# Strassen products for a pair of tiles in the last FFN chunks of a two-layer encoder

## Chip, cores and metric

One core of one Trainium2 chip. The metric is the device time of one launch in microseconds. Its engines are named as in the profile: PE (TensorE) multiplies, PEld is its weight load, DVE (VectorE) and ACT (ScalarE) work on elements, POOL (GpSimd) and SP (SyncE) issue DMA transfers among other things.

## What is computed

An inference step of an encoder with two layers. Each layer has a mixer and then a channel MLP with squared ReLU, which is the part that matters here:

```python
for i in range(DEPTH):                     # 2 layers
    ...
    h = rmsnorm(x, g_norm[i, 2]) * (1 + sc2) + sh2
    f = jnp.square(jax.nn.relu(h @ ffn_w_up[i])) @ ffn_w_down[i]
    x = x + gt2 * rmsnorm(f, g_norm[i, 3])
```

`x` has 1024 prompt rows and 32 sample rows of 1024 channels; `ffn_w_up` is 1024 x 4096 and `ffn_w_down` 4096 x 1024, in float32. The outputs are the new rows and the states of the mixers.

## The kernel before

**Tiles.** The rows lie along the free dimension in three tiles (`TILES`, L27): tiles 0 and 1 with 384 columns each, tile 2 with 256 prompt and 32 sample columns, 288 together. Channels lie on partitions, in 8 blocks of 128.

**Three products.** Each float32 operand is split into a rounded part and its remainder (`wh`, `wl` for weights, `hh`, `hl` for the input, `fh`, `fl` for the hidden part). A product of 128 x 128 weights is three matmuls: wh by the rounded input, wh by the remainder, wl by the rounded input (`products`, L929).

**Chunks and passes.** The MLP's 4096 hidden channels are cut into eight chunks of 512. `passes` (L338 to L345) lists which chunk is worked on for which tiles. In a pass, a tile has four up products of 8 blocks (96 matmuls, bank `pf`), relu and square on ACT into `r`, the split into `fh` on ACT and `fl` on DVE, and then eight down products of 4 blocks (96 matmuls, bank `pg`), each added to `acc` on DVE (`ffn_item`, L1358). The downs of one item run after the first up of the next, so PE has work while the hidden part is made. In the second layer, chunks 0 to 3 are done for one tile after the other, 4 and 5 for all three, 6 and 7 for tiles 0 and 1, and 6 and 7 of tile 2 last.

**Weights.** A chunk has eight weight items of 512 KB, four up and four down. SP loads an item into one of three `raw` buffers (`RAW_SLOTS`, L30); `do_w` (L441) copies it on ACT to `wh` and subtracts on DVE into `wl`. Both lie in slots of a ring with the tag W (`W_SLOTS`, 16 slots, so eight items). An item is prepared when the item eight before it is used up (`stream_ready`, L622). Loads of the conditioning weights, "ada", share the stream and the `raw` buffers; DVE multiplies and adds them (`aa`), and `some_ada` (L349) says how many go with which pass.

**Order around it.** The program is written out in Python: `tick` keeps an estimate of PE's time, and `weave`, `pull` and `fillers` interleave the norms, the pool mixer and the output with the passes. A scheduler then orders the instructions of each engine; each engine runs its own list in order, and SP and POOL issue their DMAs in theirs. `mix_to_ffn` (L1455) makes a tile's MLP input. `to_out` (L1659) adds the last residual of tiles 0 and 1, transposes them (`turn_out`) and stores them in 64 pieces of 48 KB (`store_out`, L1649): 40 from SP, 24 from POOL. The last statistics, the transposes and the stores of tile 2 follow its last down products.

## Time and profile before

| | |
|---|---|
| time, median of 3 runs | 2150.81 us (2150.66 to 2152.59) |
| profiled execution, span | 2150.9 us |
| mean granted TensorE clock | 0.998 |
| PE busy | 2133.6 us, 99% |
| DVE busy | 1434.0 us, 67% |
| ACT busy | 976.4 us, 45% |
| DMA | 311.79 MB, mean 145 GB/s |

The span runs from the first to the last instruction of the profiled execution. A row of a group gives source line, engine, operation, output and inputs, shape and count, then the busy time and the mean length of one in ns, then the idle time before them and what ended it. A row of the timeline gives start, length, engine, line and operation. Matmuls overlap in the array, so their lengths add up to more than the time that they take. Lengths on DVE and ACT overlap a little too where neighbours are independent.

### The profile page before, as it was taken

The numbers are of one execution on the slowest core, as the hardware profiler recorded it, in microseconds if no ns is written. First come the engines' busy times: TensorE is split into PE (matmuls) and PEld (weight loads), VectorE is DVE, ScalarE is ACT, GpSimd is POOL, SyncE is SP. The second block draws the span as 40 slices with busy tenths as digits, with TensorE's granted clock in tenths as the row PEclk, the third lists the DMA queues.
The fourth block names the chain that finished last, engine by engine and source line by source line (L and its number), as shares of the span: only waits on it lengthen the run. The fifth ranks groups of instructions, "written<-read, shape, count | busy, mean of one in ns | idle before, by whom it ended". The sixth has DMA issues, their size and how long they took to land.

```text
span 2150.9 us, 33133 instructions
## 1 busy us (share of the span) xinstructions
PE 2133.6 (99%) x13122; PEld 2071.0 (96%) x13122; DVE 1434.0 (67%) x2554; ACT 976.4 (45%) x1655; POOL 22.3 (1%) x44
## 2 busy tenths in 40 slices
PE   8999999999999999999999999999999999999998
PEld 5878999999999999999999999999999999999998
DVE  6778838567778549486757779869675554523377
ACT  5634431233456652323345566666564542313344
POOL 0000000000000000000000000000000000000003
PEclk9999999999999999999999999999999999999999
DMA  8586524353446444244545466565544542302246
GB/s 290 162 262 207 183 82 136 97 157 104 133 126 217 132 148 147 86 131 131 179 125 162 150 184 189 162 197 156 151 145 147 161 153 66 101 20 79 69 127 141
DMA packets 389360, 311.79 MB, mean 145 GB/s; under 512 B 47150, under 2 KB 352598, under 8 KB 389204
## 3 DMA queue, kind: packets, MB, share of 16 engines
q1 hardware_dynamic: 388276, 308.38, 46.9%
q8 instruction: 103, 1.69, 0.3%
q0 software_dynamic: 896, 1.28, 0.3%
q14 instruction: 53, 0.43, 0.1%
q10 hardware_dynamic: 32, 0.01, 0.0%
HBM read 278.95 MB, written 30.66 MB: 144 GB/s over the span
## 4 chain that ended last, share of the span: by engine, by line
PE 97%; DVE 1%; DMA 1%; ACT 0%; issue 0%; DVEq 0%; ACTq 0%
PE pf L934 11%; PE pf L936 11%; PE pg L934 11%; PE pf L935 11%; PE pg L935 11%; PE pg L936 11%; PE pu L934 3%; PE pu L936 3%; PE pu L935 3%; PE po L935 3%; PE po L934 3%; PE po L936 3%; PE pv L960 2%; PE pv L962 2%; PE pv L961 2%; PE psp L1288 1%
## 5 line engine op out<-in xcount | busy, mean ns | idle before, releaser
L934 PE MATMUL pg<-fh,wh_dn 128*128 128x384 f32 (+1 forms) x1536 | 495.6, 323 | 0.1
L934 PE MATMUL pf<-hh,wh_up 128*128 128x384 f32 (+1 forms) x1536 | 494.4, 322 | 0.0
L936 PE MATMUL pf<-hh,wl_up 128*128 128x384 f32 (+1 forms) x1536 | 493.0, 321 | 1.1 <-DVE wl_up L79 1.1
L935 PE MATMUL pf<-hl,wh_up 128*128 128x384 f32 (+1 forms) x1536 | 493.1, 321 | 0.0
L935 PE MATMUL pg<-fl,wh_dn 128*128 128x384 f32 (+1 forms) x1536 | 492.8, 321 | 0.0
L936 PE MATMUL pg<-fh,wl_dn 128*128 128x384 f32 (+1 forms) x1536 | 492.5, 321 | 0.0
L79 DVE TENSOR_TENSOR wl_up<-raw,wh_up 128x1024 fp32r<-128x1024 f32 x152 | 185.5, 1222 | 167.2 <-ACT wh_up L449 167.1
L936 PEld LDWEIGHTS pf<-hh,wl_up 128*128 128x128 f32 x1536 | 288.6, 188 | 1.7 <-DVE wl_up L79 1.7
L934 PEld LDWEIGHTS pg<-fh,wh_dn 128*128 128x128 f32 x1536 | 288.3, 188 | 1.8 <-ACT fh L1194 0.6
L935 PEld LDWEIGHTS pg<-fl,wh_dn 128*128 128x128 f32 x1536 | 288.3, 188 | 1.1 <-DVE fl L79 0.3
L935 PEld LDWEIGHTS pf<-hl,wh_up 128*128 128x128 f32 x1536 | 288.3, 188 | 0.4
L934 PEld LDWEIGHTS pf<-hh,wh_up 128*128 128x128 f32 x1536 | 288.2, 188 | 0.4
L449 ACT ACTIVATE wh_up<-raw 128x1024 fp32r<-128x1024 f32 x152 | 161.1, 1060 | 280.6 <-PE pf L935 214.3
L936 PEld LDWEIGHTS pg<-fh,wl_dn 128*128 128x128 f32 x1536 | 288.3, 188 | 0.0
L79 DVE TENSOR_TENSOR acc<-acc,pg 128x384 f32<-128x384 f32 (+1 forms) x336 | 173.6, 517 | 142.7 <-PE pg L936 142.3
L449 ACT ACTIVATE wh_dn<-raw 128x1024 fp32r<-128x1024 f32 x152 | 160.9, 1060 | 203.5 <-PE pg L935 170.6
L79 DVE TENSOR_TENSOR wl_dn<-raw,wh_dn 128x1024 fp32r<-128x1024 f32 x152 | 185.8, 1223 | 82.8 <-ACT wh_dn L449 82.3
L79 DVE SCALAR_TENSOR_TENSOR aa<-raw,csil,aa 128x512 f32<-128x512 f32 (+1 forms) x364 | 203.7, 618 | 5.4 <-DMA raw<-in_w_ada_dram 5.3
L1370 ACT ACTIVATE r<-pf 128x384 f32<-128x384 f32 (+1 forms) x192 | 86.5, 450 | 201.4 <-PE pf L936 182.2
L79 DVE TENSOR_TENSOR fl<-r,fh 128x384 fp32r<-128x384 f32 (+1 forms) x192 | 99.9, 520 | 82.5 <-ACT fh L1194 81.4
L934 PE MATMUL pu<-hh,wh_u 128*128 128x384 f32 (+1 forms) x384 | 126.0, 328 | 0.0
L934 PE MATMUL po<-ush,wh_o 128*128 128x384 f32 (+1 forms) x384 | 123.5, 322 | 0.0
(273 smaller groups left out, 2923.4 us busy)
## 6 DMA issues: line engine op xcount, KB each, us to landing
raw<-in_ffn_w_up_dram SPq DMA_DIRECT2D x152, 512.0 KB, 3.8
raw<-in_ffn_w_down_dram SPq DMA_DIRECT2D x152, 512.0 KB, 3.4
raw<-in_w_ada_dram SPq DMA_DIRECT2D x96, 512.0 KB, 4.1
raw<-in_sgu_w_in_dram SPq DMA_DIRECT2D x40, 512.0 KB, 3.8
xd<-acc SPq DMA_DIRECT2D x8, 1536.0 KB, 7.4
raw<-in_sgu_w_out_dram SPq DMA_DIRECT2D x24, 512.0 KB, 3.5
xo_r<-xd SPq DMA_DIRECT2D x32, 384.0 KB, 3.4
vd<-vt SPq DMA_DIRECT2D x32, 256.0 KB, 4.4
```

Source lines behind the costliest of these rows:

```text
L79: return op(out, *args, **kw)
L449: act(out=wh, in_=r, func=AF.Copy)
L934: mm(ps[:, :n], wh, rh, start=i == 0, stop=False)
L935: mm(ps[:, :n], wh, rl, start=False, stop=False)
L936: mm(ps[:, :n], wl, rh, start=False, stop=i == last)
L960: mm(ps[:m, :], a_h, wh[:, o : o + 512], start=k == 0, stop=False)
L961: mm(ps[:m, :], a_h, wl[:, o : o + 512], start=False, stop=False)
L962: mm(ps[:m, :], a_l, wh[:, o : o + 512], start=False, stop=k == KB - 1)
L1288: mm(sp[:, c * P : (c + 1) * P], vl[:, c, k * P : (k + 1) * P], wr[:, c * P : (c + 1) * P], start=True, stop=True,)
L1370: act(out=r[:, :n], in_=ps[:, :n], func=AF.Relu)
```

## The change

In the second layer, chunks 4 to 7 of tiles 0 and 1 become four passes of their own (`PAIR`), and tile 2 does all its eight chunks alone, last.

In a paired pass the up products are computed as a product of 2 x 2 blocks. The weights are cut into halves along the 1024 input channels and into two hidden blocks of 128; the two tiles are the two column blocks. Instead of eight block products of 12 matmuls there are seven (Strassen's scheme in Winograd's form), for two hidden block pairs per pass. `quad_product` is one product; four of its right sides are combinations of the tiles' inputs, made once by `combos` and `first_combo` on DVE and ACT; four left sides are combinations of weights, made from two raw items by `quads` (sums on DVE, the split on ACT and DVE; `A22` and the two halves of `S34` in parts of 512). Some products are added up in the same bank, with ACT copying out what stands there in between (`copy`: a1, a2, a3, b1), and DVE adds the parts (`r12`, `r22`, `r11`) before relu and square (`keep`). The down products are as before.

Four of the 16 weight slots are lent (`LENT`) from the last but one single pass of tile 1 on to hold combinations; other combinations take the room of tile 2's input, which is therefore made only during the down products of the last pair pass (`late_norm`). Tile 2's chunks 4 and 5 load their weights again. The ada items that went with the passes of several tiles now go with tile 1's passes 0 to 3, two each. The first layer's order stays.

```diff
@@ -27,6 +27,7 @@
 TILES = [(0, 384, 0), (384, 384, 0), (768, 256, DEC)]
 NT = len(TILES)
 W_SLOTS = 16
+LENT = 4
 RAW_SLOTS = 3
 WINDOWS = (2, 4, 8, 16)
 
...
@@ -258,6 +259,40 @@
 
 
     ada_last = {}
+
+    slots = deque(range(LENT - W_SLOTS, LENT))
+    slots.rotate(LENT)
+    lent = {"left": LENT, "called": False}
+    held = {}
+    ring = []
+
+    def w_tile(name, key=None):
+
+        i = slots.popleft()
+        if key is None:
+            slots.append(i)
+        else:
+            held.setdefault(key, []).append(i)
+        if i < 0:
+            dtype = F32 if key is None else F32R
+            return work.tile([P, 1024], dtype, tag="W", bufs=W_SLOTS - LENT, name=name)
+        dtype = F32 if key is None else F32R
+        if ring[:1] != [dtype]:
+            ring[:] = dtype, work.tile([P, LENT * 1024], dtype, tag="R", bufs=1, name=f"ring{len(ring)}")
+        return ring[1][:, i * 1024 : (i + 1) * 1024]
+
+    def w_free(key):
+        for i in held.pop(key):
+            if i >= 0 and lent["called"]:
+                lent["left"] -= 1
+            else:
+                slots.append(i)
+
+    def w_call():
+        lent["called"] = True
+        for i in [i for i in slots if i >= 0]:
+            slots.remove(i)
+            lent["left"] -= 1
 
     def add_wide(l, j):
 
...
@@ -315,13 +350,14 @@
                 )
 
     def w_chunk(n):
-        l, c, _ = passes[n]
+        l, c, tiles = passes[n]
         for j in range(4):
             f = 4 * c + j
             add_w(
                 ("up", n, j),
                 ffn_w_up[l][:, f * P : (f + 1) * P].rearrange("(k p) f -> p k f", p=P),
                 (8, P),
+                ("one", "two")[j % 2] if tiles == PAIR else "w",
             )
         for q in range(4):
             add_w(
@@ -338,11 +374,11 @@
     passes = [(0, c, [t]) for t in every for c in (0, 1)]
     passes += [(0, c, every) for c in range(2, 4)]
     passes += [(0, c, [t]) for t in every for c in range(4, 8)]
-    passes += [(1, c, [t]) for t in every for c in range(4)]
-    passes += [(1, c, every) for c in range(4, 6)]
-
-    passes += [(1, c, every[:-1]) for c in (6, 7)]
-    passes += [(1, c, [NT - 1]) for c in (6, 7)]
+    PAIR = every[:2]
+    passes += [(1, c, [t]) for t in PAIR for c in range(4)]
+    LEND_AT = ("up", len(passes) - 2, 0)
+    passes += [(1, c, PAIR) for c in range(4, 8)]
+    passes += [(1, c, [NT - 1]) for c in range(8)]
 
     rest = []
 
@@ -383,13 +419,15 @@
         w_chunk(n)
         if l == 0:
             some_ada(12 if len(tiles) > 1 else 4 if c in (4, 5) and tiles == every[:1] else 0)
-        elif len(tiles) > 1:
-            some_ada(4)
+        elif tiles == [1]:
+            some_ada(2)
     some_ada(99)
 
-    worder = [s[1] for s in stream if s[0] == "w"]
+    worder = [s[1] for s in stream if s[0] in ("w", "one", "two")]
     wpos = {k: i for i, k in enumerate(worder)}
-    wdone = set()
+    for _, key, _, _ in [s for s in stream if s[0] == "two"]:
+        for x in ("A1", "A22", "S12", "S34"):
+            wpos[("up", key[1], key[2] // 2, x)] = wpos[key]
     raws = {}
     loads = {}
     state = {"issued": 0, "next": 0, "raw": 0, "used": 0, "folds": 0}
...
@@ -438,10 +476,57 @@
             loads[key] = i.ins
             state["issued"] += 1
 
+    def w_pair(key, w=1024):
+        names = ["_".join(map(str, (x, *key))) for x in ("wh", "wl")]
+        if w == 512:
+            x = w_tile(names[0], key)
+            witem[key] = x[:, :512], x[:, 512:]
+        else:
+            witem[key] = tuple(w_tile(x, key) for x in names)
+        return witem[key]
+
+    def w_split(key, r, w=1024):
+        wh, wl = w_pair(key, w)
+        act(out=wh, in_=r, func=AF.Copy)
+        tt(out=wl, in0=r, in1=wh.bitcast(F32), op=ALU.subtract)
+
+    def quads(n, j, r1, r2):
+
+        a11, a12, a21, a22 = r1[:, :512], r1[:, 512:], r2[:, :512], r2[:, 512:]
+        key = lambda x: ("up", n, j // 2, x)
+        s3 = []
+
+        def first():
+            s3.append(work.tile([P, 512], F32, tag="aa", bufs=2, name=f"s3_{n}_{j}"))
+            tt(out=s3[0], in0=a11, in1=a21, op=ALU.subtract)
+            w_split(key("A1"), r1)
+
+        def second():
+            tt(out=a21, in0=a21, in1=a22, op=ALU.add)
+            w_split(key("A22"), a22, 512)
+
+        def third():
+            tt(out=a22, in0=a21, in1=a11, op=ALU.subtract)
+            w_split(key("S12"), r2)
+
+        def fourth():
+            tt(out=a12, in0=a12, in1=a22, op=ALU.subtract)
+            state["raw"] -= 1
+            wh, wl = w_pair(key("S34"))
+            for at, x in ((0, s3[0]), (512, a12)):
+                w = slice(at, at + 512)
+                act(out=wh[:, w], in_=x, func=AF.Copy)
+                tt(out=wl[:, w], in0=x, in1=wh[:, w].bitcast(F32), op=ALU.subtract)
+            state["raw"] -= 1
+
+        subs.extend([(2, first), (1, second), (2, third), (2, fourth)])
+
+    subs = deque()
+
     def do_w(key, r):
-        wh = work.tile([P, 1024], F32R, tag="W", bufs=W_SLOTS, name="wh_" + "_".join(map(str, key)))
-        wl = work.tile([P, 1024], F32R, tag="W", bufs=W_SLOTS, name="wl_" + "_".join(map(str, key)))
-        witem[key] = (wh, wl)
+        wh, wl = w_pair(key)
+        if key == LEND_AT:
+            w_call()
         if key == ("v", 0, 0):
             act(out=wh[:, :512], in_=r[:, :512], func=AF.Copy)
             late_hi.append(lambda: act(out=wh[:, 512:], in_=r[:, 512:], func=AF.Copy))
...
@@ -1411,6 +1506,122 @@
         pending.append(down)
 
 
+    def pair_item(p, after):
+        l, c, tiles = passes[p]
+        n = ncol[0]
+        hid = {t: [None] * 4 for t in tiles}
+        made = [0]
+
+        def keep(t, j, r, src=None):
+            if src is None:
+                src = r
+            act(out=r, in_=src, func=AF.Relu)
+            act(out=r, in_=r, func=AF.Square)
+            name = f"{l}_{c}_{t}_{j}"
+            if made[0] < 5:
+                a, b = t_hid("h", "fh" + name), t_hid("l", "fl" + name)
+            else:
+                x = work.tile([P, 768], F32R, tag="x3", bufs=3, name="fx" + name)
+                a, b = x[:, :n], x[:, n:]
+            made[0] += 1
+            split(a, b, r, n)
+            hid[t][j] = a, b
+
+        def parts(x):
+            if x > 0:
+                return combo[x]
+            t, k0 = {-11: (0, 0), -21: (0, HK), -22: (1, HK)}[x]
+            return [(hh[t][:, k0 + k, :], hl[t][:, k0 + k, :]) for k in range(HK)]
+
+        def quad_product(ps, jp, w, x, first):
+            key, at = w
+            wh, wl = need_w(("up", p, jp, key))
+            tick(12 * (0.004 + n / 2265.0))
+            for k, (rh, rl) in enumerate(parts(x)):
+                o = slice(at + k * P, at + (k + 1) * P)
+                mm(ps[:, :n], wh[:, o], rh, start=first and k == 0, stop=False, skip_group_check=True)
+                mm(ps[:, :n], wh[:, o], rl, start=False, stop=False, skip_group_check=True)
+                mm(ps[:, :n], wl[:, o], rh, start=False, stop=k == HK - 1, skip_group_check=True)
+
+        def copy(ps, name):
+            x = t_c(name)
+            act(out=x, in_=ps[:, :n], func=AF.Copy)
+            return x
+
+        def add(a, b, name):
+            r = t_m(name)
+            tt(out=r, in0=a[:, :n], in1=b[:, :n], op=ALU.add)
+            return r
+
+        def up(jp):
+            name = f"{l}_{c}_{jp}"
+            j = 2 * jp
+
+            def done(key):
+                w_finish(("up", p, jp, key))
+
+            pa, pb = ps_ms(f"pfa{name}"), ps_up(f"pfb{name}")
+            quad_product(pa, jp, ("A1", 0), -11, True)
+            a1 = copy(pa, f"a1{name}")
+            weave()
+            if jp == 0:
+                flush()
+                finish("combos")
+            quad_product(pb, jp, ("S12", 0), 1, True)
+            b1 = copy(pb, f"b1{name}")
+            weave()
+            quad_product(pa, jp, ("S12", 512), 2, False)
+            done("S12")
+            a2 = copy(pa, f"a2{name}")
+            weave()
+            quad_product(pb, jp, ("S34", 512), -22, False)
+            keep(1, j, add(a2, pb, f"r12{name}"))
+            weave()
+            quad_product(pa, jp, ("S34", 0), 3, False)
+            done("S34")
+            a3 = copy(pa, f"a3{name}")
+            keep(1, j + 1, add(a3, b1, f"r22{name}"))
+            weave()
+            pc = ps_up(f"pfc{name}")
+            quad_product(pc, jp, ("A1", 512), -21, True)
+            done("A1")
+            keep(0, j, add(a1, pc, f"r11{name}"))
+            weave()
+            quad_product(pa, jp, ("A22", 0), 4, False)
+            done("A22")
+            keep(0, j + 1, t_m(f"r21{name}"), pa[:, :n])
+            weave()
+
+        def down():
+            sts = {}
+            for q in range(4):
+                wh, wl = need_w(("dn", p, q))
+                for t in reversed(tiles):
+                    for d in (2 * q, 2 * q + 1):
+                        ps = ps_dn(f"pg{l}_{c}_{t}_{d}")
+                        terms = []
+                        for j in (0, 1, 3, 2) if t == 1 else range(4):
+                            o = j * 256 + (d % 2) * P
+                            a, b = hid[t][j]
+                            terms.append((wh[:, o : o + P], wl[:, o : o + P], a[:, :n], b[:, :n]))
+                        products(ps, n, terms)
+                        accumulate(t, d, ps, False)
+                        if after is not None:
+                            if d == 0:
+                                sts[t] = Stat(t, f"rf{l}_{t}")
+                            sts[t].square(d)
+                        if d % 2 == 1 and t == tiles[0]:
+                            w_finish(("dn", p, q))
+                        weave(d % 2)
+            for t in tiles if after is not None else ():
+                after(sts[t])
+
+        up(0)
+        up(1)
+        if after is not None:
+            fillers.append(late_norm.pop())
+        down()
+
     last_ps = {}
 
     def rows_last(part, name):
@@ -1461,7 +1672,76 @@
             for a in range(4):
                 nc.sync.dma_start(xtd[:, a], acc[t][32 * a : 32 * a + 32, :, HALO:])
         need_ada(l, 4)
+        if l == 1 and t == NT - 1:
+            got = []
+            yield from out[0].finish(got)
+            late_norm.append((f"ffn1_{t}", apply(t, 1, 2, 3, got[0])))
+            fillers.append(("combos", combos()))
+            return
         yield from modulate(out[0], l, 2, 3)
+
+    late_norm = []
+    combo = {}
+    HK = KB // 2
+
+    def both(t, k):
+
+        return hh[t][:, k : k + 2, :].bitcast(F32), hl[t][:, k : k + 2, :].bitcast(F32)
+
+    def t_two(name):
+        return t_x(name, [P, 768]).rearrange("p (k n) -> p k n", k=2)
+
+    def keep_parts(x, out):
+        for i, (h, l) in enumerate(out):
+            act(out=h, in_=x[:, i, :], func=AF.Copy)
+            tt(out=l, in0=x[:, i, :], in1=h.bitcast(F32), op=ALU.subtract)
+
+    def combos():
+
+        while lent["left"]:
+            yield 1.0
+        units = []
+        for tag, n in (("R", 5), ("hh2", 3), ("hl2", 3)):
+            x = work.tile([P, n, 2, 384], F32R, tag=tag, bufs=1, name=f"combo_{tag}")
+            units += [(x[:, i, 0], x[:, i, 1]) for i in range(n)]
+        units.append(
+            (
+                work.tile([P, 384], F32R, tag="rr", bufs=2, name="combo_rr"),
+                late.tile([P, 384], F32R, tag="wg", bufs=1, name="combo_wg"),
+            )
+        )
+        for i in (2, 3, 4):
+            combo[i] = units[4 * i - 8 : 4 * i - 4]
+        combo[1] = [(hh[1][:, k], hl[1][:, k]) for k in range(HK)]
+        for k in (0, 2):
+            x, y, z = (t_two(f"combo_{v}{k}") for v in "xyz")
+            tt(out=x, in0=both(1, k)[0], in1=both(1, k)[1], op=ALU.add)
+            tt(out=y, in0=both(1, HK + k)[0], in1=both(1, HK + k)[1], op=ALU.add)
+            yield True
+            tt(out=z, in0=y, in1=x, op=ALU.subtract)
+            keep_parts(z, combo[3][k : k + 2])
+            yield True
+            tt(out=z, in0=both(0, k)[0], in1=both(0, k)[1], op=ALU.add)
+            tt(out=x, in0=x, in1=z, op=ALU.subtract)
+            yield True
+            tt(out=y, in0=y, in1=x, op=ALU.subtract)
+            keep_parts(y, combo[2][k : k + 2])
+            yield True
+            tt(out=z, in0=both(0, HK + k)[0], in1=both(0, HK + k)[1], op=ALU.add)
+            tt(out=z, in0=z, in1=y, op=ALU.subtract)
+            keep_parts(z, combo[4][k : k + 2])
+            yield False
+
+    def first_combo():
+
+        for k in (0, 2):
+            x, z = (t_two(f"combo1_{v}{k}") for v in "xz")
+            tt(out=x, in0=both(1, k)[0], in1=both(1, k)[1], op=ALU.add)
+            tt(out=z, in0=both(0, k)[0], in1=both(0, k)[1], op=ALU.add)
+            yield True
+            tt(out=x, in0=x, in1=z, op=ALU.subtract)
+            keep_parts(x, combo[1][k : k + 2])
+            yield False
 
     def to_ffn0(st):
         fillers.append((f"ffn0_{st.t}", mix_to_ffn(st, 0)))
...
@@ -1624,12 +1904,24 @@
         for p, (pl, c, tiles) in enumerate(passes):
             if pl != l:
                 continue
+            if tiles == PAIR:
+                if p > 0 and passes[p - 1][2] != PAIR:
+                    paired()
+                pair_item(p, after if c == 7 else None)
+                continue
             for t in tiles:
                 if c == 0:
                     if any(f[0] == f"ffn{l}_{t}" for f in fillers):
                         flush()
                     finish(f"ffn{l}_{t}")
                 ffn_item(p, t, after if c == 7 else None)
+
+    def paired():
+
+        def stages():
+            yield from first_combo()
+
+        fillers.append(("combos", stages()))
 
     run_ffn(0, to_pool)
 
```

More of the change, by code (lines that the diff above doesn't have):

```diff
@@ L239, in tile_stream_encoder_step, with add_w @@
     witem = {}
-    def add_w(key, ap, shape):
-        stream.append(("w", key, ap, shape))
+    def add_w(key, ap, shape, kind="w"):
+        stream.append((kind, key, ap, shape))
     def add_ada(l, j):
@@ L424, in issue @@
             else:
-                r = work.tile([P, 1024], F32, tag="W", bufs=W_SLOTS, name=f"raw{k}")
+                r = w_tile(f"raw{k}")
             if kind == "x" and key < 6:
@@ L625, in stream_ready @@
             return False
-        if stream[k][0] == "w":
-            i = wpos[stream[k][1]] - W_SLOTS // 2
-            return i < 0 or worder[i] in wdone
-        return True
+        if subs:
+            return len(slots) >= subs[0][0]
+        return stream[k][0] not in ("w", "one", "two") or len(slots) >= 2
     def stream_step():
+        if not subs and stream[state["next"]][0] == "one":
+            issue()
+            state["next"] += 1
         k = state["next"]
@@ L636, in stream_step @@
         run_deferred()
+        if kind == "two":
+            if not subs:
+                quads(key[1], key[2], raws.pop(k - 1), raws.pop(k))
+            subs.popleft()[1]()
+            if not subs:
+                state["next"] += 1
+            issue()
+            return
         r = raws.pop(k)
@@ L656, in stream_waits @@
         kind, key = stream[state["next"]][:2]
-        if kind == "w":
+        if kind in ("w", "one", "two"):
             return bool(fillers) and wpos[key] > state["used"] + 5 and time["dve"] > time["pe"] + 1.0
@@ L675, in w_finish @@
     def w_finish(key):
-        wdone.add(key)
+        w_free(key)
     fillers = deque()
```

1 line of the change is left out of this document (added).

## The prediction

> **What bounds the kernel now.** I read the page's first two parts, then the windows of the second layer, then the timeline of single matmuls.
>
> ```profile
> span 2150.9 us, 33133 instructions
> PE 2133.6 (99%) x13122; PEld 2071.0 (96%) x13122; DVE 1434.0 (67%) x2554; ACT 976.4 (45%) x1655; POOL 22.3 (1%) x44
> PEclk9999999999999999999999999999999999999999
> PE 97%; DVE 1%; DMA 1%; ACT 0%; issue 0%; DVEq 0%; ACTq 0%
> ```
>
> The chain that ended last is TensorE's at full clock. Each window's columns are its length, the busy times of PE, PEld, DVE, ACT and POOL, then the clock, the DMA share and GB/s:
>
> ```profile
> 1500.00:1600.00 100.00, 99.88 (x563) 97.44 (x562) 69.27 (x126) 56.83 (x100) 0.00 (x0) 1.00 0.53 159
> 1600.00:1700.00 100.00, 100.00 (x635) 100.00 (x634) 58.15 (x90) 51.59 (x86) 0.00 (x0) 1.00 0.47 143
> 1900.00:2000.00 100.00, 100.00 (x624) 100.00 (x623) 31.47 (x48) 29.03 (x49) 0.00 (x0) 1.00 0.16 49
> 2000.00:2100.00 100.00, 100.00 (x600) 100.00 (x599) 58.99 (x93) 46.02 (x76) 0.00 (x0) 1.00 0.39 110
> ```
>
> PE is full, so no wait is left there to gain from, and a new wait adds its whole length. VectorE and ScalarE have a third to two thirds free.
>
> The length of one matmul is no price: matmuls overlap. One 384-column matmul is shown as 335 ns, but the distance between starts is what counts:
>
> ```profile
> L934 PE MATMUL pf<-hh,wh_up 128*128 128x384 f32 x1024 | 343.1, 335 | 0.0
> ...
> 1572.27 0.33 PE L934 MATMUL pf<-hh,wh_up 128*128 128x384 f32 x1
> ...
> 1579.90 0.33 PE L936 MATMUL pf<-hh,wl_up 128*128 128x384 f32 x1
> ...
> 2094.99 0.30 PE L934 MATMUL pf<-hh,wh_up 128*128 128x288 f32 x1
> ...
> 2096.99 0.29 PE L934 MATMUL pf<-hh,wh_up 128*128 128x288 f32 x1
> ```
>
> Start to start it is 44 steps in 7.63 us, 0.1734 us, for 384 columns; for tile 2's 288 columns 15 steps in 2.00 us, 0.1333 us.
>
> **What goes from TensorE.** A plain pass has 96 up matmuls per tile, 192 for two tiles. A paired pass has two halves of seven products of 12 matmuls, 168. Four passes save 4 x 24 = 96 matmuls of 384 columns, 96 x 0.1734 = **16.65 us**. (By the 335 ns it would be 32 us, which counts the overlap twice.) Tile 2's matmuls are moved, not changed: 0. The last norm and its stores still follow tile 2's last product with the same instructions: 0.
>
> The Trainium skill, "TensorE: Matmul & The Clock Gate", part 1, puts the start-to-start time of a warm matmul at N / 2.4 GHz + about 2.5 ns, 162.5 ns for 384 columns. The row's 173.4 ns does not agree, and decides; by the page the saving would be an estimated 15.6 us.
>
> **What is added on the other engines.** Here too the distance between starts is shorter than the shown length, where the next instruction does not need the last one's result:
>
> ```profile
> 1434.66 0.55 DVE L79 TENSOR_TENSOR fl<-r,fh 128x384 fp32r<-128x384 f32 x1
> 1435.13 1.22 DVE L79 TENSOR_TENSOR wl_up<-raw,wh_up 128x1024 fp32r<-128x1024 f32 x1
> 1436.27 0.75 DVE L79 TENSOR_TENSOR sq_r_2x<-sq_r_2x 128x576 f32<-128x576 f32 x1
> 1436.94 1.22 DVE L79 TENSOR_TENSOR wl_up<-raw,wh_up 128x1024 fp32r<-128x1024 f32 x1
> ...
> 1435.68 1.06 ACT L449 ACTIVATE wh_up<-raw 128x1024 fp32r<-128x1024 f32 x1 [0.22 <-PE pf L935]
> 1436.65 0.47 ACT L1370 ACTIVATE r<-pf 128x384 f32<-128x384 f32 x1
> 1437.15 0.52 ACT L1372 ACTIVATE r<-r 128x384 f32<-128x384 f32 x1
> 1437.71 0.52 ACT L1194 ACTIVATE fh<-r 128x384 fp32r<-128x384 f32 x1
> 1438.13 0.56 ACT L1617 ACTIVATE acc<-pp,vec 128x384 f32<-128x384 f32 x1
> ```
>
> DVE: 0.47 us for 384 elements, 1.14 for 1024, 0.67 for 576. ACT: 0.97 for 1024, 0.42 for 384 when independent, 0.5 to 0.56 when it needs the one before. No row shows 512 elements of these kinds: I take 0.60 on DVE and 0.53 on ACT (bounds 0.47 to 0.67 and 0.42 to 0.97). 768 on DVE lies between 0.67 and 1.14; I take 0.87.
>
> DVE gains 16 weight remainders (1.14), 56 half-weight sums and remainders (0.60), 40 additions and remainders of 384 (0.47) and 22 sums of 768 (0.87): 18 + 34 + 19 + 19 = 90 us. ACT gains 16 copies of 1024 (0.97), 24 of 512 (0.53) and 48 of 384 (about 0.45): 16 + 13 + 22 = 51 us. In the four windows above DVE is idle for 182 of 400 us and ACT for 216, so the sums fit; their cost is 0 unless something is late where PE needs it. Sixteen more loads of 512 KB, since tile 2 reads chunks 4 and 5 again, fall into windows with a DMA share of 0.16 to 0.53: 0 as well. Eight ada blocks moved into tile 1's passes 0 to 3 and the 12 instead of 16 weight slots from pass 2 on: the built order puts them just in time there (the latest weight remainder ends within 0.2 us of the matmul that reads it). 0, upper bound 2 us for one load coming late (loads and stores with their time to landing, then SP's timeline with the stores' start and length):
>
> ```profile
> raw<-in_ffn_w_up_dram SPq DMA_DIRECT2D x152, 512.0 KB, 3.8
> raw<-in_ffn_w_down_dram SPq DMA_DIRECT2D x152, 512.0 KB, 3.4
> out_dram<-y_sq SPq DMA_DIRECT2D x33, 48.0 KB, 2.1
> ...
> 2118.13 26.38 SPq L1657 DMA_DIRECT2D out_dram<-y_sq  x40
> ```
>
> **The new waits, place by place.** I listed the instructions of each engine in the built order of the changed kernel, and for each matmul that waits I added what stands ahead on the engine it waits for. A hand-over is read from four rows:
>
> ```profile
> 1800.99 0.33 PE L936 MATMUL pg<-fh,wl_dn 128*128 128x384 f32 x1
> ...
> 1801.36 0.55 DVE L79 TENSOR_TENSOR acc<-acc,pg 128x384 f32<-128x384 f32 x1 [1.52 <-PE pg L936]
> ...
> 2142.11 0.44 ACT L763 ACTIVATE sq_rf<-acc 128x288 f32<-128x288 f32 x1 [1.04 <-DVE acc L79]
> ...
> 2142.61 0.74 PEld L1677 LDWEIGHTS pn_last<-ones,sq_rf 128*128 128x128 f32 x6 [0.21 <-ACT sq_rf L763]
> ```
>
> DVE or ACT starts 0.37 us after the last matmul of a sum starts, and PE's part 0.06 us after the other engine ends.
>
> 1. Last pass of tile 1 to the first pair pass: the hidden part of the last item stands behind a new 512 copy on ACT. r 0.47, square 0.52, copy 0.53, fh 0.52, the hand-overs and gaps 0.37 + 0.1 from the start of the last up matmul, 2.5 us in all, against 13 starts, 2.25 us: 0.25 us.
>
> 2. First half of the first pair pass. The combination of the halves overwrites tile 1's input, which the last up products still read, so it cannot be done early. After the last down product DVE has one accumulation (0.47), four sums of 768 (3.48), two half-weight sums (1.20), one weight remainder (1.14) and three remainders of 384 (1.41), 7.7 us. It starts about 0.5 us late, behind a sum before it, and with the hand-over PE gets the first of the new operands after 8.3 us, where it has 43 matmuls, 7.46 us: 0.9 us. Two results later ACT starts a weight copy of 1024 (0.97), and the copy of product two (0.48), on which product four waits in the same bank, stands behind it: 0.37 + 0.97 + 0.48 + 0.06 us from the start of a matmul which stands two starts, 0.35 us, ahead of product four: 1.53 us. Together **2.45 us**.
>
> 3. In the other pair passes the copy that frees the bank for product three of the second half stands behind eleven ACT instructions. With 0.42 us between independent ones it ends 0.3 us early, with the full 0.52 us 0.7 us late. I take 0.15 for each of three passes, 0.45, and 0.5 at the last pass, where the input of tile 2 is normalised between: 0.95 us. Bounds: -0 and 0.7 in each of eight halves, 5.6 us.
>
> 4. Tile 2, chunk 5 to chunk 6. The remainder of its fourth down weight is queued on DVE behind the accumulation of the product just before the matmuls that read it: 0.34 + 0.37 + 1.22 + 0.06 = 1.99 us from the start of that product's last matmul against five starts, 0.67 us; the next weight comes 1.14 us behind it against seven starts, 0.93 us. 1.32 + 0.21 = **1.5 us**, where 0.34 and 0.37 are DVE's start and spacing for 288 columns, an estimate from the 0.37 and 0.47 of the 384-column rows.
>
> 5. The other chunk starts of tile 2 come out within 0.2 us; I take 0.1 in all, and up to 0.5 for each of seven as a bound, 3.5 us.
>
> Sum: 0.25 + 2.45 + 0.95 + 1.5 + 0.1 = 5.25 us given back. Against the profiled execution, 2150.9 - 16.65 + 5.25 = **2139.5 us**. That execution's span is 0.1 us above the median of the runs, 2150.81, which changes nothing. Bounds: with no wait 2134.25; lower is excluded, since PE has no idle time left to lose; with all upper bounds (2 + 0.25 + 4 + 5.6 + 3 + 3.5) 2152.6.
>
> **Rivals.**
>
> *The waits are hidden.* If the scheduler's slack covers nearly all of them, 2134.3 to 2136.5, about 2135.5. For it: before, the same kind of hand-over runs without a gap in all windows. Against: the two queues of places 2 and 4 have no other work between.
>
> *Every half of a pair pass waits.* The seven products are shorter (2.08 us) than a plain product (4.16 us), while relu, square and split of a half (twelve ACT instructions, 6 us) and its weight copies (5.5 us of 1.06, 0.97 and 0.53 parts) and four new copies fill about 13 of 14.6 us of ACT. Each late copy stops PE. At 1.2 us in each of eight halves it gives back 9.6 us more: 2149. Against it: half of the ACT time lies outside, under the down products.
>
> *Slower: stores ahead of weights on SP.* The outputs of tiles 0 and 1 were stored last, with no load behind them; now 24 stores of the x40 row stand in one run on SP ahead of the load of chunk 5's fourth down weight and three loads of chunk 6. From the matmul that releases the weight slot before them, PE has 218 matmuls, 29.1 us; copy, remainder, load and copy of the weights around the run take 8 us, so a store may take 0.88 us. The row has 26.38 / 40 = 0.66, which leaves 5 us of slack. Each store waits for the transfer eight before it, and some of those are now 512 KB loads, and POOL stores into the same outputs; at 1.75 us each PE loses 21 us, 2160. It costs anything from 0.88, and more than the change wins from 1.35.
>
> The Trainium skill, "TensorE: Matmul & The Clock Gate", part 1, adds that the clock falls to half after about 3.4 us without work, so that one long wait would cost more than itself. None of the waits of the forecast is that long, the clock row shows no such fall, and by that rule only this rival gets dearer, which is an estimate.
>
> *The change does not do what it says*: if the products were not dropped, PE's count would not fall; the built order has 96 matmuls less, so I give it nothing.
>
> **How the numbers follow.** Forecast, 2136.5 to 2146.5: 0.59. Hidden: 0.10. Every half waits, 2146.5 to 2155: 0.14. Slower by the stores or a queue that I have not seen, 2155 and up: 0.17. A measurement can tell 0.2%, 4.3 us, from no change: faster below 2146.5, slower above 2155.1. So faster 0.69, same 0.14, slower 0.17. The range 2134 to 2156 takes in all the bounds and leaves out the upper case; the likeliest case's own range is 2136.5 to 2146.5.
>
> **What would show it.** PE records fall by about 96 with the start-to-start times unchanged. PE's idle time names VectorE or ScalarE in front of the second and fourth products of the first pair pass, about 2.5 us, and VectorE's wl_dn in tile 2 before the chunk where the stores end, about 1.5 us; elsewhere under 1 us per pass. SP's run of 24 stores lasts about 16 us. Gaps of over 0.5 us in each pair half, ended by ACT's copies, would prove the second rival; a PE wait ended by a weight load in tile 2 the third. Windows under full clock would make all of it wrong.

## The result and the profile after

| | before | after |
|---|---|---|
| time, median of 4 runs each | 2150.98 us (2150.66 to 2152.59) | 2141.86 us (2141.37 to 2143.43) |
| profiled execution, span | 2150.9 us | 2139.6 us |
| PE instructions | 13122 | 13026 |

The ratio is 0.9958, with a 95% interval of 0.9943 to 0.9972: faster by 9.1 us, with the interval 6.0 to 12.3 us. The forecast was 2139.5.

First the head of the page after, span and busy times:

```profile
span 2139.6 us, 33156 instructions
PE 2119.9 (99%) x13026; PEld 2054.6 (96%) x13026; DVE 1521.5 (71%) x2688; ACT 1018.0 (48%) x1743; POOL 22.3 (1%) x44
```

PE has exactly the 96 matmuls less that were counted. DVE is busy 87.5 us longer and ACT 41.6 us; the sums were 90 and 51 us. Where this lies is seen in two of the windows that were shown for the kernel before (length, then busy times of PE, PEld, DVE, ACT, POOL, then clock, DMA share, GB/s):

```profile
1600.00:1700.00 100.00, 97.84 (x563) 95.74 (x562) 93.37 (x151) 52.90 (x93) 0.00 (x0) 1.00 0.43 130
2000.00:2100.00 100.00, 98.83 (x737) 97.66 (x737) 58.27 (x79) 51.07 (x79) 0.00 (x0) 1.00 0.65 179
```

PE was full there before; now 2.16 us are open between 1600 and 1700 us, where DVE is at 93%, and 1.17 us between 2000 and 2100 us. The view of PE's waits from 1640 us to the end of the products, which leaves out idle times of up to 0.15 us, has three rows (who waited for whom, us in total, times, longest):

```profile
PE pfb L1542 <- ACT b L1548: 1.4, 1, 1.4
PE pg L1031 <- DVE wl_dn L80: 1.2, 1, 1.2
PE pfb L1543 <- DVE hl L80: 0.7, 1, 0.7
```

Each waited once, not once per pass. The timeline of single matmuls has the places (start, length, operation, and in brackets idle time and its releaser):

```profile
1676.81 0.34 PE L1544 MATMUL pfa<-hh,wl_up_A 128*128 128x384 f32 x1
1677.86 0.44 PE L1543 MATMUL pfb<-hl,wh_up_S 128*128 128x384 f32 x1 [0.72 <-DVE hl L80]
...
1678.67 0.34 PE L1544 MATMUL pfb<-hh,wl_up_S 128*128 128x384 f32 x1
1680.41 0.44 PE L1542 MATMUL pfb<-hh,wh_up_S 128*128 128x384 f32 x1 [1.40 <-ACT b L1548]
...
1733.15 0.33 PE L1542 MATMUL pfa<-hh,wh_up_A 128*128 128x384 f32 x1
...
1795.69 0.33 PE L1542 MATMUL pfa<-hh,wh_up_A 128*128 128x384 f32 x1
...
2021.12 0.30 PE L1030 MATMUL pg<-fl,wh_dn 128*128 128x288 f32 x1
2022.57 0.40 PE L1031 MATMUL pg<-fh,wl_dn 128*128 128x288 f32 x1 [1.15 <-DVE wl_dn L80]
```

Read them start to start. Two pairs in the first pair pass: 1.05 and 1.74 us where 0.1734 is normal, so 0.88 and 1.57 us are lost (place 2). The pair in tile 2: 1.45 us for 0.1333, 1.32 us lost (place 4). Between them is a steady pair pass: from the first matmul of one pass to that of the next it is 62.54 us, where 168 up and 192 down matmuls at 0.1734 make 62.42. In the middle passes almost nothing waits.

**Two spans do not start alike.** The span fell by 11.3 us and the medians by 9.1. A statistic of the second layer's mixer, ahead of all that the change touches, starts in the two PE timelines, before and then after, at:

```profile
1419.98 0.59 PE L808 MATMUL pn_rf<-sc_rf,ones 128*128 128x288 f32 x1
```

```profile
1418.37 0.59 PE L903 MATMUL pn_rf<-sc_rf,ones 128*128 128x288 f32 x1
```

So 1.6 us of the 11.3 come from a start that happened to be earlier (the last section shows where they arise). From this matmul to the end it is 730.9 us before and 721.2 after, 9.7 us less: 16.65 less for the dropped matmuls and 7.0 more. That profiles of one place differ by up to 2 us is seen in the other runs below too, so they are compared from this matmul on.

### The profile page after: what moved, and what is told of

It reads as the page before. It is cut to its first block, busy times and chain, and to the rows that moved or that the text cites. A ratio compares the mean times of both kernels' runs of the same rounds, so it can differ in the third digit from the quotient of the medians.

```text
span 2139.6 us, 33156 instructions
## 1 busy us (share of the span) xinstructions
PE 2119.9 (99%) x13026; PEld 2054.6 (96%) x13026; DVE 1521.5 (71%) x2688; ACT 1018.0 (48%) x1743; POOL 22.3 (1%) x44
## 5 line engine op out<-in xcount | busy, mean ns | idle before, releaser
L1029 PE MATMUL pg<-fh,wh_dn 128*128 128x384 f32 (+1 forms) x1240 | 397.8, 321 | 0.1
L1031 PE MATMUL pg<-fh,wl_dn 128*128 128x384 f32 (+1 forms) x1240 | 395.8, 319 | 1.2 <-DVE wl_dn L80 1.2
L1030 PE MATMUL pg<-fl,wh_dn 128*128 128x384 f32 (+1 forms) x1240 | 396.0, 319 | 0.0
L1029 PE MATMUL pf<-hh,wh_up 128*128 128x384 f32 (+1 forms) x1000 | 318.1, 318 | 0.0
L1031 PE MATMUL pf<-hh,wl_up 128*128 128x384 f32 (+1 forms) x1000 | 316.6, 317 | 0.1
L1030 PE MATMUL pf<-hl,wh_up 128*128 128x384 f32 (+1 forms) x1000 | 316.7, 317 | 0.0
L1031 PEld LDWEIGHTS pf<-hh,wl_up 128*128 128x128 f32 x1000 | 188.0, 188 | 0.8 <-DVE wl_up L80 0.8
L1029 PEld LDWEIGHTS pf<-hh,wh_up 128*128 128x128 f32 x1000 | 187.6, 188 | 0.6 <-ACT wh_up L534 0.2
L1030 PEld LDWEIGHTS pf<-hl,wh_up 128*128 128x128 f32 x1000 | 187.7, 188 | 0.3
L80 DVE TENSOR_TENSOR ring<-raw,ring 128x1024 fp32r<-128x1024 f32 x69 | 84.2, 1222 | 44.2 <-ACT ring L534 44.2
```

Source lines behind the costliest of these rows:

```text
L80: return op(out, *args, **kw)
L1029: mm(ps[:, :n], wh, rh, start=i == 0, stop=False)
L1030: mm(ps[:, :n], wh, rl, start=False, stop=False)
L1031: mm(ps[:, :n], wl, rh, start=False, stop=i == last)
```

## The experiments

Each kernel ran in turn with the kernel before on the same chip. The table has, for each, the ratio of times, then what was read from its trace: the start of that mixer statistic, the time from there to the end of the span, and the "wait sum": for every matmul of an MLP product (`pf` or `pg`) in that part, what the distance to the next start has over 0.1734 us (384 columns) or 0.1333 us (288), where it is over 0.08 us. The kernel before took 2152.28 us beside runs 1, 2, 3 and 5 and 2151.05 us beside runs 4, 6 and 7, so kernels of different groups are compared by their ratios or by the rest, not by their times.

| kernel | time, us | ratio to before (95%) | span | from | rest | wait sum | rest less waits |
|---|---|---|---|---|---|---|---|
| before | 2150.98 | | 2150.9 | 1419.98 | 730.9 | 3.3 | 727.6 |
| after | 2141.86 | 0.9958 (0.9943 to 0.9972) | 2139.6 | 1418.37 | 721.2 | 9.5 | 711.8 |
| 1, plain products in the new order | 2160.51 | 1.0038 (1.0023 to 1.0053) | 2157.8 | 1418.72 | 739.0 | 11.5 | 727.6 |
| 2, stores on POOL | 2141.30 | 0.9949 (0.9934 to 0.9964) | 2139.0 | 1420.08 | 718.9 | 7.2 | 711.7 |
| 3, one copy on POOL | 2142.18 | 0.9957 (0.9943 to 0.9972) | 2139.9 | 1419.43 | 720.5 | 9.0 | 711.5 |
| 4, tile 1's stores twice | 2148.34 | 0.9985 (0.9975 to 0.9995) | 2148.9 | 1420.27 | 728.6 | 17.1 | 711.6 |
| 5, ada with the pair passes | 2140.35 | 0.9945 (0.9930 to 0.9960) | 2138.8 | 1420.42 | 718.4 | 6.9 | 711.5 |
| 6, both 2 and 5 | 2136.26 | 0.9930 (0.9918 to 0.9943) | 2134.5 | 1418.80 | 715.7 | 4.2 | 711.5 |
| 7, 1 with stores on POOL | 2151.32 | 0.9999 (0.9989 to 1.0008) | 2149.9 | 1419.42 | 730.5 | 3.0 | 727.5 |

The last column falls into two groups: 727.5 to 727.6 us with eight block products, 711.5 to 711.8 with seven. Everything else that separates the nine kernels is in the column of waits.

### 1. The new order of passes with plain products

The pair passes of the changed kernel compute their up products as eight block products; the seven products, the lent slots and the late input of tile 2 go.

```diff
-                ("one", "two")[j % 2] if tiles == PAIR else "w",
+                "w",
...
-    LEND_AT = ("up", len(passes) - 2, 0)
+    LEND_AT = None
...
-        if l == 1 and t == NT - 1:
+        if False:
...
-            if tiles == PAIR:
+            if False:
```

> Order alone: the same passes as the changed kernel, but the pair passes use the plain eight block products, with no combinations and no lent slots in use. Theory (the gain is the 96 matmuls, the new order only costs): about 13 us above the changed kernel and 0 to 3 us above the one before, with one wait of about 1.3 us on wl_dn in tile 2 after the run of stores and none at the start of the pair passes. Rival (the order itself gains, the dropped products gain little because the pair passes wait): within 5 us of the changed kernel.

It was 8.2 us slower than before, where 0 to 3 were expected, and by the rest 17.8 us above the changed kernel, where about 13 were expected. The window from 2000 to 2060 us and the waits from 1640 us on:

```profile
2000.00:2060.00 60.00, 54.96 (x404) 53.49 (x403) 31.75 (x43) 27.10 (x41) 0.00 (x0) 1.00 0.67 181
```

```profile
PE pg L1029 <- ACT fh L1289: 1.5, 1, 1.5
PE pf L1029 <- ACT wh_up L534: 1.5, 1, 1.5
PE pg L1031 <- DVE wl_dn L80: 1.2, 1, 1.2
PE pg L1030 <- DVE fl L80: 0.9, 1, 0.9
```

PE loses 5 us in tile 2, behind the stores of tile 1. From the timelines of SP, DVE and ACT:

```profile
1999.75 14.41 SPq L1949 DMA_DIRECT2D out_dram<-y_sq  x23
2014.27 1.52 SPq L474 DMA_DIRECT2D raw<-in_ffn_w_down_dram  x3
2028.57 6.79 SPq L474 DMA_DIRECT2D raw<-in_ffn_w_up_dram  x4
...
2024.69 2.94 ACT L534 ACTIVATE wh_dn<-raw 128x1024 fp32r<-128x1024 f32 x3
...
2027.32 3.49 DVE L80 TENSOR_TENSOR wl_dn<-raw,wh_dn 128x1024 fp32r<-128x1024 f32 x3
...
2032.65 1.06 ACT L534 ACTIVATE wh_up<-raw 128x1024 fp32r<-128x1024 f32 x1 [5.02 <-DMA raw<-in_ffn_w_up_dram]
```

Three down loads stand behind the stores and land between 2018.3 and 2021.1 us. Their copies come on ACT only from 2024.69 on, behind work that waits for PE, though ACT was idle for 1.83 us twice since 2018.4; their remainders come from 2027.32 on and hold the three `raw` buffers, the first of them until about 2028.5. The next up load starts at 2028.57, which fits that release, and its copy ends after PE needed it. So the third rival's queue is at work, loads late behind a run of stores, with a smaller price than it was given and in a kernel without Strassen's products, but the order of ACT's and DVE's lists adds to it. It is not settled by this run alone how much belongs to the order of passes and how much to the stores; run 7 settles that.

The last two waits, 1.5 us in front of the matmul at 2058.59 and 0.9 us in front of that at 2059.88, have a price of their own: the clock column (third from the end) falls to 0.50 right behind them.

```profile
2060.38:2063.79 3.41, 3.41 (x17) 3.41 (x16) 2.26 (x4) 3.03 (x5) 0.00 (x0) 0.50 0.59 187
```

Fourteen distances in this stretch are 0.24 us instead of 0.1333, 1.5 us of the loss.

### 2 and 3. The stores, and one weight copy, on POOL

Run 2 issues the 40 stores of tiles 0 and 1 that SP had from POOL:

```diff
-                    store_out(0, nc.sync, range(4, KB))
+                    store_out(0, nc.gpsimd, range(4, KB))
...
-                store_out(1, nc.sync, range(6))
+                store_out(1, nc.gpsimd, range(6))
```

> The 40 stores of tiles 0 and 1 that SP issued are issued by POOL instead; all else as in the changed kernel. Theory (the wait in tile 2 comes from the order that the run of 24 stores on SP gives to the weights): the gap of 1.3 us on wl_dn disappears, the gaps of 0.9 and 1.6 us at the start of the first pair pass stay; 1.0 to 2 us faster. Rival (it is the number of weight slots that makes the weight late): the gap stays within 0.3 us, time the same.

The wait for `wl_dn` is gone, the two of the first pair pass stand:

```profile
PE pfb L1542 <- ACT b L1548: 1.4, 1, 1.4
PE pfb L1543 <- DVE hl L80: 0.7, 1, 0.7
PE pg L1030 <- DVE fx L80: 0.2, 1, 0.2
```

DVE makes that remainder at 2007.51 us here, ahead of the next chunk's up weights, where it came at 2021.29 in the kernel after. The rest falls by 2.3 us and the wait sum by as much; 1 to 2 us were expected. The ratios, 0.9949 and 0.9958, differ by 1.9 us, and their intervals overlap.

Run 3 takes the copy that stood ahead of product two's copy off ACT:

```diff
+        elif key == ("dn", passes.index((1, 4, PAIR)), 0):
+            nc.gpsimd.tensor_copy(wh, r)
```

> In the first pair pass the rounded copy of the first down weight is made on POOL instead of ACT. Theory (product four waits because the bank's copy stands behind this weight copy on ACT): the gap of 1.57 us at the fourth product falls to 0.6 to 0.8 us, what the hand-over alone takes; the gap of 0.88 us before it stays; 0.8 to 1 us faster. Rival (the gap is the hand-over through the bank and the combinations): it stays at 1.4 us or more.

The wait in front of the fourth product falls to 0.6 us (a loss of 0.75 in place of 1.57), as it must if the weight copy was what held it:

```profile
1680.69 0.44 PE L1544 MATMUL pfb<-hh,wh_up_S 128*128 128x384 f32 x1 [0.58 <-ACT b L1550]
```

The time did not follow: a new loss of 0.38 us opens at 1685.47, in front of a matmul that waits for ACT's next copy `a`, and the ratio, 0.9957, is that of the changed kernel, 0.9958, where 0.8 to 1 us were expected. The rest in the trace is 0.7 us shorter. So the cause of the 1.57 us is shown in the trace, but as an improvement of the time it is not: this edit gives nothing that these runs can measure.

### 4. The stores of tile 1 twice

SP issues tile 1's 24 stores a second time, so the run in front of the loads doubles.

```diff
                 store_out(1, nc.sync, range(6))
+                store_out(1, nc.sync, range(6))
```

> The 24 stores that stand in one run on SP are issued twice, 48 in a run, so 13.9 us more of SP; the results are the same. Theory (the run has cover: the weight behind it was loaded and copied 7 to 8 us before PE used it, so a run longer than that must show): 5 to 8 us slower than the changed kernel, with a PE wait that ends with a weight copy on ACT at tile 2's chunk 5 or 6. Rival (the run is not in the way of anything, SP has time enough): the time within 1 us of the changed kernel.

SP's timeline, of the kernel after and of this one:

```profile
1994.63 13.89 SPq L1949 DMA_DIRECT2D out_dram<-y_sq  x24
```

```profile
1996.41 27.27 SPq L1949 DMA_DIRECT2D out_dram<-y_sq  x48
2023.78 0.42 SPq L474 DMA_DIRECT2D raw<-in_ffn_w_down_dram  x1
```

its PE timeline where chunk 5's last down weight is first read, with two matmuls further on, ACT's copy of this weight, and one window:

```profile
2022.37 0.30 PE L1031 MATMUL pg<-fh,wl_dn 128*128 128x288 f32 x1
2028.60 0.61 PE L1029 MATMUL pg<-fh,wh_dn 128*128 128x288 f32 x1 [5.93 <-ACT wh_dn L534]
...
2032.18 0.45 PE L1030 MATMUL pf<-hl,wh_up 128*128 128x288 f32 x1
2032.42 0.45 PE L1031 MATMUL pf<-hh,wl_up 128*128 128x288 f32 x1
...
2027.49 1.06 ACT L534 ACTIVATE wh_dn<-raw 128x1024 fp32r<-128x1024 f32 x1 [13.27 <-DMA raw<-in_ffn_w_down_dram]
```

```profile
2030.00:2031.00 1.00, 1.00 (x5) 1.00 (x6) 0.93 (x1) 0.03 (x1) 0.00 (x0) 0.50 0.68 116
```

ACT was idle for 13.27 us until the load behind the stores landed, so here it is SP that holds PE. The run of stores grew by 13.4 us and PE lost 6.1 us (start to start 6.23 for 0.1333), so 7.3 us were covered. That fits the kernel after, where there are 7.4 us: ACT's copy of this weight ends at 2013.57 (the row is below, under place 4), and its first reader starts at 2020.99. The forecast's threshold, 0.88 us per store, gives 24 x (27.27 / 24 - 0.88) = 6.1 us as well. The run is slower than the changed kernel by 7.4 us of the rest and by 5.8 us of the ratios, within the 5 to 8 expected.

The wait has a second price. After it the clock stands at 0.50 and the matmuls are 0.24 us apart, until 2034.8 us. The Trainium skill, "TensorE: Matmul & The Clock Gate", part 1, says that the clock falls to half after about 3.4 us without work and rises after as long a busy time; here the fall agrees, and the slow stretch of 6.2 us was longer than that. Run 1 differs: its clock fell behind idle times of 1.5 and 0.9 us with one matmul between them, so a fall does not need one unbroken wait of that length.

### 5 and 6. The ada items elsewhere

Run 5 gives the eight ada items to the first two pair passes, four each, in place of tile 1's passes. Run 6 joins this with the stores of run 2.

```diff
-        elif tiles == [1]:
-            some_ada(2)
+        elif tiles == PAIR:
+            some_ada(4 if c < 6 else 0)
```

> The eight ada items of tile 1's passes 0 to 3 go with the pair passes of chunks 4 and 5 instead, four each. Theory (the combinations come late at the first pair pass because VectorE is full in the passes before): both gaps at its start, 0.88 and 1.57 us, go or fall under 0.3 us, no pair pass gains a gap of over 0.5 us, and the time falls by 1.5 to 2.5 us. Rival (the combinations are late because they overwrite what the last up products read, whatever else VectorE does): the gaps stay within 0.3 us of what they were.

The two waits at the start of the pair passes are gone in run 5, and that for `wl_dn` stays; the rest falls by 2.8 us, a little more than the 1.5 to 2.5 expected. The reason is in DVE's timeline. The kernel after, and then run 5:

```profile
1639.44 2.73 DVE L80 SCALAR_TENSOR_TENSOR aa<-raw,csil,aa 128x512 f32<-128x512 f32 x4
...
1672.24 1.02 DVE L80 TENSOR_TENSOR hl<-combo_x,hh 128x384 fp32r<-128x384 f32 x2
...
1677.25 1.03 DVE L80 TENSOR_TENSOR hl<-combo_x,hh 128x384 fp32r<-128x384 f32 x2
```

```profile
1650.17 1.03 DVE L80 TENSOR_TENSOR hl<-combo_x,hh 128x384 fp32r<-128x384 f32 x2
...
1651.59 1.02 DVE L80 TENSOR_TENSOR hl<-combo_x,hh 128x384 fp32r<-128x384 f32 x2
```

With the ada sums in front, DVE makes the combinations of the input until 1678 us, when PE is at the second product; without them it is done at 1652.6 us, as the last up products of tile 1 end (the last of them starts at 1651.90).

> The ada items in the pair passes of chunks 4 and 5 and all stores of tiles 0 and 1 on POOL, together. Theory (two separate waits, each with its own cause): no gap of over 0.5 us in the second layer beyond those that the kernel before has too, 3.5 to 4 us less than the changed kernel, some 13 us less than the one before, 2137 to 2139. Rival (what one place gains is lost at the next): at or above the time of the moved ada items alone.

Run 6 has none of the three waits, its view of PE's waits from 1640 us to the end of the products is empty, and it is the fastest kernel: 2136.26 us, 14.8 us or 0.70% under the kernel before (0.57% to 0.82%). By the rest it is 5.5 us under the changed kernel, more than the 3.5 to 4 expected and about the 2.3 and 2.8 of runs 2 and 5 together. Its windows at the places of the waits:

```profile
1600.00:1700.00 100.00, 100.00 (x577) 99.74 (x577) 79.25 (x126) 52.62 (x90) 0.00 (x0) 1.00 0.36 111
...
2000.00:2100.00 100.00, 100.00 (x757) 100.00 (x756) 58.64 (x79) 51.90 (x79) 22.57 (x37) 1.00 0.63 186
```

### 7. The new order with plain products and the stores on POOL

The edits of run 1 and those of run 2.

> Order alone with the plain eight products, as in the first experiment, and all stores of tiles 0 and 1 on POOL. Theory (the 8 us that the order alone lost are the place of the stores on SP in front of weights, nothing of the order of the passes): the waits of 1.3, 1.6, 1.7 and 1.2 us in tile 2 go, the time is within 2 us of the kernel before, and 13 to 16 us above the changed kernel with the stores on POOL. Rival (tile 2 alone at the end is what costs): still 5 us or more above the kernel before.

The same time as before, 0.9999, and the window in which run 1 lost 5 us is full:

```profile
2000.00:2060.00 60.00, 60.00 (x456) 60.00 (x455) 35.40 (x50) 31.46 (x48) 20.97 (x34) 1.00 0.66 192
```

So the new order, with its reloaded chunks and moved ada items, costs nothing that these runs can measure by itself when products are plain, and the whole loss of run 1 hung on where the stores are issued, with the order of the lists that goes with it. Run 2 has the same order of passes, ada items and stores with seven products. Run 7 less run 2 is 11.6 us by the rest, less than the 13 to 16 expected, since run 2 keeps the waits at the start of the pair passes; without the wait sums of both it is 15.8. Run 7 less run 6 is 15.1 us (by the rest, 14.8): what the seven products are worth when those waits are gone, of the 16.65 us of dropped matmuls.

## Why the prediction was right, step by step

**The saving.** 96 matmuls at 0.1734 us, 16.65 us. The groups of the last column differ by 15.7 to 16.1 us. A rest of 0.5 to 0.9 us is spread over gaps below 0.08 us, such as the 0.12 us by which a pair pass is longer than its 360 starts; the rows do not show what sets it. The 32 us of the shown lengths do not appear, and the added 129 us on DVE and ACT cost nothing but the waits below.

**Place 1**, 0.25 expected: 0.6 us in three pieces, 0.16, 0.32 and 0.12 us. The row with x2 holds two matmuls, and the end of a remainder on DVE comes just ahead of the next:

```profile
1651.65 0.77 PE L1029 MATMUL pg<-fh,wh_dn 128*128 128x384 f32 x2
1652.47 0.46 PE L1544 MATMUL pfa<-hh,wl_up_A 128*128 128x384 f32 x1
...
1651.20 1.22 DVE L80 TENSOR_TENSOR wl_up_A<-raw,wh_up_A 128x1024 fp32r<-128x1024 f32 x1
```

The 0.32 us are a wait for the first pair pass's own weight remainder, which ends at 1652.42; the forecast had no such wait, only that of the hidden part.

**Place 2**, 0.9 and 1.53 expected: 0.88 and 1.57, and 0.11 after each when PE starts again. (8.3 less 7.46 is 0.84, which the forecast put at 0.9.) The sizes of the forecast were right, but its reason was wrong in one point. It said that the combinations cannot be made early, since the last up products read the input, and it put the moved ada blocks at 0. The first is true, but it leaves time: run 5 makes these combinations at 1650 to 1652.6 us, as those products end and well ahead of need, while in the changed kernel the ada sums in tile 1's passes fill DVE. The moved ada items are what place 2 costs. The built order from which the sum was made held this queue, so the sum came out right without it.

**Place 3**, 0.95 expected with a bound of 5.6: 0.5 us in all, the excesses over 0.08 us from 1686 to 1890 us. ACT copies in time in every steady half, so the 0.15 us per middle pass did not come.

**Place 4**, 1.5 expected: 1.32 us, and three excesses of 0.1 us after it. The rows of ACT and DVE in the kernel after have the cause in order:

```profile
2012.51 1.06 ACT L534 ACTIVATE wh_dn<-raw 128x1024 fp32r<-128x1024 f32 x1
...
2020.92 0.46 DVE L80 TENSOR_TENSOR acc<-acc,pg 128x288 f32<-128x288 f32 x1 [1.12 <-PE pg L1031]
2021.29 1.22 DVE L80 TENSOR_TENSOR wl_dn<-raw,wh_dn 128x1024 fp32r<-128x1024 f32 x1
```

The rounded weight is there at 2013.57. Its remainder could start, and DVE is idle for 1.12 us before the accumulation, but the remainder stands behind that accumulation in DVE's list, and PE waits until 2022.51. It is the order that waits, not the work, and run 2, in whose order the remainder comes earlier, has no such wait. The next weight's 0.21 us did not come.

**Place 5**, 0.1 expected: four starts of tile 2's chunks have about 0.3 us each, 1.3 us together, where the kernel before has 0.4 at its one such start. This term was too small by 0.8 us.

Sum of the five places: 0.6 + 2.67 + 0.5 + 1.6 + 0.9 = 6.3 us for 5.25. The wait sums, 9.46 less 3.33, say 6.1. With what lies below 0.08 us it is 7.0, and so the change was worth 9.7 us, not 11.4. The upper bounds of 4 and 3 us that the forecast gave places 2 and 4 had no working; they were not reached.

**The span's agreement is luck.** The forecast of 2139.5 and the span of 2139.6 agree because the early start of 1.6 us made up for the 1.7 us more given back. The forecast also took the span before, 2150.9, as 0.1 us above the median time, but a span is not a time: in every execution with both on record the span is 1.7 to 2.0 us the shorter (2139.6 for 2141.37 us). So the execution that was profiled before took some 2152.7 us, like the slowest of its runs (2152.59). By the medians the change was worth 9.1 us, and the forecast gain of 11.4 was 2.3 us too large.

**The rivals.** That the waits are hidden (2135.5) is refuted by the three rows of waits; run 6 shows what it would have taken. That every half of a pair pass waits (2149) is refuted by the steady pass. The rival on the slow side, stores ahead of weights, is a true mechanism: run 4 makes it stop PE for 6.1 us, and run 1 loses 8.2 us with the stores on SP, 1.5 of them by the clock. It did not decide here because a store took 13.89 / 24 = 0.58 us of SP, far from 0.88; the cover is 7.3 us, not the 5 that the forecast's 0.66 left. That 0.66 was read wrongly: the row of 40 stores before holds a pause of 3.8 us, as two narrower windows show, and its two parts took 0.58 and 0.55 us a store.

```profile
2118.13 9.35 SPq L1657 DMA_DIRECT2D out_dram<-y_sq  x16
...
2131.29 13.21 SPq L1657 DMA_DIRECT2D out_dram<-y_sq  x24
```

The 1.75 us per store of its price was not seen.

## What to carry to other kernels

When a change drops matmuls from a full TensorE, price them by the distance between starts, then list for each matmul that follows a rearranged stretch what stands ahead of its operand on the in-order queue of the engine that makes it; here that gave the three waits of over half a microsecond to within 0.1 us, and it missed smaller ones, 1.2 us in places 1 and 5. Ask of every such queue whether work that nobody needs yet, like the ada sums, could stand elsewhere: moving it together with the stores won 5.5 us on top of the 9.7 of the change, by the rest. A plain version of the new order, with the old arithmetic, tells the price of the order from the gain of the arithmetic, and it found a loss of 8 us to the place of the stores, of which the changed kernel has 2.3 (run 2).

## What the runs showed that was not expected

Executions of one kernel differ by 0.6 to 4.4 us, 3.0 in the 21 of the kernel before. In the nine profiles up to 2 us of difference is there before the first matmul of interest: the mixer statistic starts between 1418.37 and 1420.42 us, with the same number of matmuls ahead of it. A good part of it is the clock near the start of the span. From 18.5 to 22 us, before and then after:

```profile
18.50:22.00 3.50, 3.50 (x10) 2.69 (x9) 1.54 (x4) 2.85 (x7) 0.00 (x0) 0.51 1.09 386
```

```profile
18.50:22.00 3.50, 3.50 (x18) 2.84 (x17) 1.58 (x4) 3.15 (x7) 0.00 (x0) 1.00 1.09 385
```

The kernel before has 10 matmuls there at a clock of 0.51, the kernel after 18 at 1.00. Ahead of this stretch the same matmul starts 0.3 us earlier in the kernel before, behind it 1.3 us later, which is the 1.6 us of the spans. Runs 4, 5 and 7 have such a stretch as well and lose 1.4 to 1.6 us in it; the other four do not. Run 2, without one, starts late by a wait of 0.9 us near 1353 us and smaller ones, whose cause stays open. Differences below 2 us are better read from a common matmul on than from spans.

In run 4 a wait of 6.1 us halved the clock for 6.2 us after it, which cost nearly half its own length again: the 24 matmuls from 2028.60 to 2034.80 would take 3.2 us at 0.1333 us each, 3.0 us less, and 24 x (0.24 - 0.1333) = 2.6 of these are the clock's. The wait for `wl_dn` that the kernel after has at the same place, 1.32 us, disappears in it, and the rest is 7.4 us longer in all.
